# The first two row blocks of V by float32 products, in an encoder block on one core

## The chip, the core and the metric

The kernel runs on one core of one Trainium2 chip. The core has five engines with queues of their own: TensorE (PE, matrix products and transposes into PSUM banks), VectorE (DVE), ScalarE (ACT), GpSimd (POOL) and SyncE (SP, which here only issues DMAs). Each engine works through its queue in order and waits at an instruction whose inputs are not there. The metric is the device time of one execution in microseconds (us), lower is better; a kernel is given by the median of several executions.

## The reference

One encoder block over 1024 tokens of 1024 channels, all float32. The input projection comes first, and only its V part is changed; Q and K come directly behind it.

```python
u = rms_norm(x, norm1_g)                    # x * rsqrt(mean(x*x) + 1e-6) * g
proj = u @ w_in                             # 1024 x 1024 by 1024 x 5120
q, k, v, cb, cc, ch, ga, gb = split(proj)   # 512, 512, 512, 3 x 512, 2 x 1024 columns
q = rms_norm(q by heads of 64, q_norm_g)
k = rms_norm(k by heads of 64, k_norm_g)
y_a = neighbourhood_attention(q, k, v, rpb) @ w_attn_branch
y_b = short_gated_conv(cb, cc, ch, conv_w) @ w_conv_branch
x = x + (sigmoid(ga) * y_a + sigmoid(gb) * y_b) @ w_o
x = x + square(relu(rms_norm(x, norm2_g) @ w_mlp_in)) @ w_mlp_out
```

## The kernel before

**Numbers in two parts.** Every float32 operand of a product is scaled by a power of two and split into two float16 parts, a high part and the remainder, the low part. A product is then three f16 passes (`PASSES`, HH, HL, LH: high by high, high by low, low by high); low by low is left out. For the weights, ACT makes the high part from the raw tile with a per-partition scale (in `v_part`, L555, for V; in `Chunk.prep`, L306, for all others) and DVE the low part (L297 for the chunks). The scale is a power of two from the largest magnitude of the weights, or from the sum of their squares: `v_scale`, `pow2`, `pow2_half`. ACT's squares of the weights for that sum are at L266.

**The normalised input.** `x` is read in eight blocks of 128 rows (`load_x`, L366). For a block, `norm` lets ACT square it and add up along the row (L433), `rstd` makes the inverse root: DVE forms the mean (`tensor_scalar`), ACT takes `Sqrt`, and four DVE steps follow (a reciprocal and one Newton step, the last at L415). Then the high part `u[:, 0]` is made, by POOL for blocks 1 to 7 (L437) and by ACT for block 0 (L439), and the low part by DVE. `u` must lie with channels on the partitions for the products; that tile is `uT` ([128, 2, 8, 1024] f16: part, channel block, token). Blocks 0 to 2 get there by PE transposes of f16 tiles (`turn_row`, L525, eight per part, into a PSUM bank, then a copy by ACT or DVE); blocks 3 to 7 by one transposing DMA each (`ln_turn`, L444), issued by SP.

**The V stage.** V's weights are two halves of 256 columns (`cV[0]`, `cV[1]`). For blocks 0 to 2 the products are of 128 x 256 (`v_mms`, L571), 24 for a block and a half, interleaved by hand with the steps that make their operands (the order at L585 to L720: `ln_step(b)` advances the norm of a block by one step, `v_part` makes weight parts, `tick` and `step` advance the background and foreground work). `v_post` (L579) moves a finished bank to `vT`. Blocks 3 to 7 are units of 24 products of 128 x 512 (`v_unit`, issued at L210 by `unit`; its evacuation by ACT at L516). `units[0]` counts finished units, and `apart(mark)` holds back a step of the background work until so many units are issued.

**Behind it.** Sixteen units follow, Q for blocks 0 to 7 and K for blocks 0 to 7, each 24 products of 128 x 512 at L210. The evacuation of each is `qk_vec`: ACT copies it with a scale (L736), ACT squares, `rstd` (its `Sqrt` at L407), DVE products, an f16 split. Meanwhile the parts of the next weights are made. `sforms` prepares sums for a later stage (the gates): for each pair of x blocks (n, n + 4) ACT scales both with their inverse root (L482) and POOL makes four sums of 128 x 512 (L486), sixteen in all; ACT then makes their f16 high part (L491) and DVE the low part. `SFORM` lists which pair comes at which unit count. Behind these stand conv, attention, the gates, the output projection and the MLP, none of which the change touches.

**Queues and buffers.** SP's queue holds, in order, the loads of x, of the raw weights (`load_upto`, five raw buffers) and the transposing DMAs. PSUM has three `d`, three `s` and two `o` banks. At the start ACT runs one `Sqrt` on a single column, `warm`, which loads the table of that function (L371).

Of the kernel before, what the change touches and what calls it, by code (L numbers as in the profile page):

```python
# [18 lines left out]
D = 1024  # L19
# [33 lines left out]
def encoder_block(ctx: ExitStack, tc: tile.TileContext, x, weights, cols, gqk, rel, masks, out):  # L53
# [25 lines left out]
    sc = base.tile([128, 512], F32, name="sc")  # L79
    sci = sc.bitcast(I32)  # L80
    area = {"keep": [0, 0, 144], "prep": [144, 144, 240], "tmp": [240, 240, 512]}
# [163 lines left out]
    class Chunk:  # L245
# [9 lines left out]
        def prep(self):  # L255
# [5 lines left out]
            if self.kind in "QKCG":  # L261
                self.parts = wsp.tile([128, 2, tot], F16, name="w16_ws", tag="ws")
                for p, (k, w) in enumerate(self.widths):
                    while len(self.raw) <= p:
                        yield WAIT
                    A.activation(self.parts[:, 1, :k * w].bitcast(BF16), self.raw[p][:, :k * w], AF.Square,  # L266
                                 accum_out=sc[:, at(rm, p)])
# [103 lines left out]
    A.activation(sc[:, warm], sc[:, warm], AF.Sqrt)  # L371
# [14 lines left out]
    ident = w1p.tile([128, 128], F16, name="ident", bufs=1)  # L386
    G.iota(idi, pattern=[[1, 128]], base=0, channel_multiplier=-1)
    V.tensor_scalar(ident, idi, 0.0, None, op0=OP.is_equal)
# [40 lines left out]

    def norm(xin, sq, u, y, pool):  # L430
# [4 lines left out]
        yield from rstd(ss, D, y, 9)  # L435
# [35 lines left out]
    turned, formed = [0], [0]  # L471
    SFORM = ((6, 0, 0), (7, 1, 0), (9, 2, 0), (9, 0, 1), (10, 3, 0), (10, 1, 1), (12, 2, 1), (13, 3, 1))

    def sforms():

        for mark, n, split in SFORM:
            yield from apart(mark, 0)
            pair = xt[:, n:n + 5:4]
            if not split:
                assert turned[0] >= n + 5  # L480
# [15 lines left out]
    def sform_store(n, v):  # L496
        yield from apart(units[0], 1)
        A.dma_start(GS[:, n], v)
        formed[0] = n + 1
# [10 lines left out]

    def v_unit(b, ticks):
        ps = bank("ds"[b % 2])

        def post():
# [4 lines left out]
                        for k in range(8) for sa, sw in PASSES]), post, 0, ticks)  # L519

    def turn_row(b, s):

        pt = bank16("o")
        for k in range(8):
            T.transpose(pt[:, k * 128:(k + 1) * 128], u16[:, b, s, k * 128:(k + 1) * 128], ident)  # L525

        def copy():
            o, i = UT[:, s, :, b * 128:(b + 1) * 128], pt.rearrange("p (k t) -> p k t", k=8)
            if s == 0:
                A.activation(o, i, AF.Copy)  # L530
            else:
                V.tensor_copy(o, i)
        return copy
# [5 lines left out]
    def v_sum(ch, c):  # L539
        ch.sum = bank("o")  # L540
# [8 lines left out]
    def v_part(ch, s, ks):  # L549
        for k in ks:  # L550
# [5 lines left out]
            else:  # L556
                V.scalar_tensor_tensor(lo, raw, c, hi, op0=OP.mult, op1=OP.subtract)
                if k % 4 == 3:
                    done[0] += 1
                    if ch.half == 0:  # L560
                        load_upto(done[0] + 5)

    vps, vn = {}, {}

    def v_mms(b, j, ks, *passes):
        if (b, j) not in vps:
            vps[b, j], vn[b, j] = bank("ds"[b % 2 if b < 2 else j]), 0
        for k in ks:
            for sa, sw in passes:
                n = vn[b, j] = vn[b, j] + 1  # L570
                T.matmul(vps[b, j][:, :256], UT[:, sa, k, b * 128:(b + 1) * 128],  # L571
                         vhome[0][:, j, sw, k * 256:(k + 1) * 256], start=n == 1, stop=n == 24)
        if n == 24:
            units[0] += 1

    def v_post(b, j, s):
        hi, lo = (VT[:, b, w, 256 * j:256 * j + 256] for w in range(2))
        if s == 0:
            A.activation(hi, vps[b, j][:, :256], AF.Copy, scale=2.0 ** -20)  # L579
        else:  # L580
            V.scalar_tensor_tensor(lo, vps[b, j][:, :256], 2.0 ** -20, hi, op0=OP.mult, op1=OP.subtract)
# [10 lines left out]
    ln_step(0, 7)  # L592
    for k, n in (0, 4), (4, 2), (6, 2):
        V.tensor_reduce(sc[:, at(v0.rm, k, n)], v0.raw[k // 4][:, k % 4 * 256:(k % 4 + n) * 256].rearrange(
            "p (k w) -> p k w", k=n), axis=AX, op=OP.max, apply_absolute_value=True)
    turn_row(0, 0)()
    mul(v0.rm, g1, v0.rm)
    V.tensor_reduce(sc[:, v0.a], sc[:, v0.rm], axis=AX, op=OP.max, apply_absolute_value=True)
    c = ones_col()
    V.tensor_copy(c, sc[:, v0.a])  # L600
    v_sum(v0, c)
    ln_step(1)
    v_scale(v0, 1e-30, pow2(v0.b, 14, v0.s, v0.inv, False, v0.more))
    ln_step(0)
    v_part(v0, 0, range(3))
    ln_step(1)
    v_part(v0, 0, range(3, 8))
    ln_step(1, 5)
    v_mms(0, 0, (0, 1), HH)
    turn_row(0, 1)()  # L610
    v_part(v0, 1, lower)
    v_mms(0, 0, range(2, 7), HH)
    copy = turn_row(1, 0)
    v_mms(0, 0, (7,), HH)
    copy()
    v_mms(0, 0, eight, LH)
    v_mms(0, 0, lower, HL)
    ln_step(2)
    ln_step(1)
    v_mms(1, 0, eight, HH)  # L620

    def v1_square(p):
        A.activation(v1.parts[:, 1, 1024 * p:1024 * p + 1024].bitcast(BF16), v1.raw[p], AF.Square,
                     accum_out=sc[:, at(v1.rm, p)])

    v_part(v0, 1, (4,))
    ln_step(2)
    v1_square(0)
    v1_square(1)
    ln_step(3)  # L630
    v_part(v0, 1, (5,))
    ln_step(2, 5)
    turn_row(1, 1)()
    v_mms(0, 0, (4, 5), HL)
    v_mms(1, 0, range(6), HL)
    v_part(v0, 1, (6, 7))
    v_mms(1, 0, eight, LH)
    copy = turn_row(2, 0)
    V.tensor_reduce(sc[:, v1.a], sc[:, at(v1.rm, 0, 2)], axis=AX, op=OP.add)
    c = ones_col()  # L640
    V.tensor_tensor(c, sc[:, v1.a], sc[:, gm2], op=OP.mult)
    v_sum(v1, c)
    v_mms(0, 0, (6, 7), HL)
    v_mms(1, 0, (6, 7), HL)
    copy()
    v_scale(v1, 1e-36, pow2_half(v1.b, 14, v1.s, v1.inv, v1.more))
    v_part(v1, 0, lower)
    ln_step(2)
    v_mms(2, 0, eight, HH, HL)
    ln_step(3)  # L650
    v_part(v1, 0, (4, 5))
    v_part(v1, 1, (0, 1))
    copy = turn_row(2, 1)
    ln_step(3, 5)
    copy()
    v_part(v1, 0, (6, 7))
    for b in 0, 1:
        v_mms(b, 1, lower, HH, LH)
    v_mms(2, 0, eight, LH)
    v_mms(2, 1, lower, HH, LH)  # L660
    v_part(v1, 1, (2, 3))
    ln_step(4)
    v_post(0, 0, 0)
    v_post(1, 0, 0)
    ln_step(3)
    ln_turn(u16[:, 3], 3, UT)
    push(cQ)
    ln_step(4)
    v_part(v1, 1, (4, 5))
    tick()  # L670
    ln_step(5)
    ln_step(4, 5)
    for b in range(3):
        v_mms(b, 1, upper, HH, LH)
    v_part(v1, 1, (6, 7))
    v_post(2, 0, 0)
    v_post(0, 0, 1)
    ln_step(4)
    ln_turn(u16[:, 0], 4, UT)
    load_upto(8)  # L680
    turned[0] = 5
    ln_step(5)
    tick()
    ln_step(6)
    v_post(1, 0, 1)
    v_post(2, 0, 1)
    ln_step(5, 5)
    tick()
    for ks in lower, (4, 5), (6, 7):
        for b in range(3):  # L690
            v_mms(b, 1, ks, HL)
    ln_step(6)
    ln_step(5)
    ln_turn(u16[:, 1], 5, UT)
    load_upto(done[0] + 5)
    turned[0] = 6
    ln_step(7)
    for b in range(3):
        v_post(b, 1, 0)
        v_post(b, 1, 1)  # L700
    ln_step(6, 5)
    tick()
    ln_step(7)
    ln_step(6)
    ln_turn(u16[:, 2], 6, UT)
    turned[0] = 7
    ln_step(7, 5)
    tick()
    fg.append(qk_gain())
    fg.append(sforms())  # L710
    step(2)
    for b in range(3, 8):
        v_unit(b, 8)
        if b == 3:
            ln_step(7)
            ln_turn(u16[:, 3], 7, UT)
            turned[0] = 8
        step(2)
    settle()
# [1224 lines left out]
```

## Time and profile before

| what | value |
|---|---|
| median of 3 executions | 1207.19 us (1207.16 to 1207.37) |
| span of the profiled execution | 1205.3 us |
| own time of the profiled execution | not listed; the median lies 1.9 us above the span |
| PE busy | 1188.0 us, 99% |
| DVE busy | 938.7 us, 78% |
| ACT busy | 759.8 us, 63% |
| POOL busy | 433.1 us, 36% |

The profile is one execution, in microseconds from its start. Its page gives the busy time of each engine, the span in forty slices (each digit is the busy share in tenths; PEclk is the clock granted to PE, in tenths of full speed), the chain of work that ended last, and the costliest groups of instructions. The timeline lists each engine's instructions by line, operation and tiles; `out<-in` names the tiles, `x24` says that 24 like instructions are taken together, and the brackets give the idle time of the engine just before and what ended it.

### The profile page before, as it was taken

How to read it: one execution, taken by the hardware profiler on the slowest of the kernel's cores; microseconds unless marked ns; L12 is line 12 of the kernel's file. 1: busy time of each engine (PE TensorE's matmuls, PEld its weight loads, DVE VectorE, ACT ScalarE, POOL GpSimd, SP SyncE). 2: the span in 40 equal slices, each digit the busy share in tenths (PEclk: the TensorE clock that was granted, in tenths of full speed). 3: DMA queues.
4: the chain of work that ended last, by engine and by line, in shares of the span. 5: the costliest groups of instructions: out<-in, count | busy, mean ns of one | idle time of the engine just before them, and what ended most of it. 6: DMA issues, size and time to landing. Idle time of an engine off the chain costs nothing.

```text
span 1205.3 us, 17076 instructions
## 1 busy us (share of the span) xinstructions
PE 1188.0 (99%) x6294; PEld 573.8 (48%) x6294; DVE 938.7 (78%) x1759; ACT 759.8 (63%) x1183; POOL 433.1 (36%) x280
## 2 busy tenths in 40 slices
PE   6999999999999999999999999999999999999998
PEld 4444445555444444444467444444444444444444
DVE  7777988988368787877878655545548999999997
ACT  7766679867554545337779778678676744746440
POOL 1640011222311112001004465565567471553662
PEclk9999999999999999999999999999999999999999
DMA  7766657676542211224386545445465925334202
GB/s 264 151 213 141 140 119 130 133 146 123 103 123 65 67 56 53 70 93 187 57 155 183 182 159 192 149 139 193 145 247 201 352 97 217 129 138 194 105 35 105
DMA packets 171012, 173.36 MB, mean 144 GB/s; under 512 B 131504, under 2 KB 132016, under 8 KB 166832
## 3 DMA queue, kind: packets, MB, share of 16 engines
q1 hardware_dynamic: 170352, 168.07, 47.9%
q10 hardware_dynamic: 576, 4.19, 0.8%
q8 instruction: 49, 0.80, 0.3%
q14 instruction: 35, 0.29, 0.1%
HBM read 102.51 MB, written 37.75 MB: 116 GB/s over the span
## 4 chain that ended last, share of the span: by engine, by line
PE 73%; DVE 9%; ACT 1%; issue 1%; DMA 1%; DVEq 0%; ACTq 0%
PE ps_d L210 26%; PE ps_s L210 23%; PE ps_o L210 16%; PE ps_d L1039 6%; DVE w_s L1163 2%; PE ps_o L1016 1%; PE ps_s L959 1%; DVE sg L1279 1%; DVE P L999 1%; DMA u2T<-v 1%; DVE sz L973 1%; ACT w_s L1167 0%; DVE sc L317 0%; DVE m L1281 0%; ACT sg L1245 0%
## 5 line engine op out<-in xcount | busy, mean ns | idle before, releaser
L210 PEld LDWEIGHTS <-ops 128*128 128x128 f16 x1356 | 132.4, 98 | 157.3
L210 PEld LDWEIGHTS <-w 128*128 128x128 f16 x1368 | 132.8, 98 | 140.0 <-DMA u2T<-v 0.6
L1039 PE MATMUL ps_d<-uT,w_ws 128*128 128x512 f16 x528 | 123.7, 379 | 0.1
L210 PE MATMUL ps_d<-ops 128*128 128x512 f16 (+1 forms) x528 | 118.3, 374 | 0.0
L1765 ACT ACTIVATE ops<-hf,sc 128x2048 f16<-128x2048 f32 x26 | 52.0, 2000 | 97.9 <-PE ps_o L210 35.2
L210 PE MATMUL ps_s<-ops 128*128 128x512 f16 x492 | 112.9, 379 | 0.0
L1152 POOL TENSOR_TENSOR tsum<-raw 128x512 f32<-128x512 f32 x28 | 46.0, 1658 | 149.6 <-ACT raw L1138 141.6
L1345 POOL TENSOR_TENSOR as<-as 128x512 f32<-128x512 f32 x56 | 77.5, 1384 | 39.3 <-ACT as L1625 36.0
L210 PEld LDWEIGHTS <-w_s 128*128 128x128 f16 x588 | 56.8, 98 | 69.4 <-DVE w_s L1163 1.9
L210 PE MATMUL ps_d<-u2x,w 128*128 128x512 f16 (+1 forms) x360 | 80.0, 372 | 0.0
L210 PEld LDWEIGHTS <-uT 128*128 128x128 f16 x504 | 49.0, 98 | 59.6 <-DMA uT<-u 0.8
L1039 PEld LDWEIGHTS <-w_ws 128*128 128x128 f16 x528 | 51.2, 98 | 54.5 <-DVE cv L861 0.4
L210 PE MATMUL ps_o<-ops 128*128 128x512 f16 x336 | 77.1, 379 | 0.0
L1767 DVE SCALAR_TENSOR_TENSOR ops<-hf,sc,ops 128x2048 f16<-128x2048 f32 x26 | 74.0, 2846 | 3.7 <-ACT ops L1765 3.7
L210 PE MATMUL ps_o<-u2T,w 128*128 128x512 f16 (+1 forms) x324 | 71.7, 371 | 0.0
L1138 ACT ACTIVATE raw<-raw,sc 128x256 f32<-128x256 f32 x172 | 71.0, 493 | 0.8 <-DMA raw<-in_weights 0.7
L1152 POOL TENSOR_TENSOR gsum<-raw 128x512 f32<-128x512 f32 x14 | 19.0, 1376 | 133.0 <-issue 72.8
L1167 ACT ACTIVATE w<-raw,sc 128x512 f16<-128x512 f32 (+1 forms) x28 | 24.6, 927 | 54.1 <-DVE sc L426 54.1
L297 DVE SCALAR_TENSOR_TENSOR w_ws<-raw,sc,w_ws 128x512 f16<-128x512 f32 (+2 forms) x72 | 51.2, 763 | 4.7 <-ACT w_ws L306 4.7
L1658 DVE TENSOR_TENSOR as<-ps_d,as 128x512 f32<-128x512 f32 (+1 forms) x14 | 9.4, 672 | 55.8 <-ACT as L1677 53.4
L210 PE MATMUL ps_s<-u2T,w 128*128 128x512 f16 (+1 forms) x252 | 52.7, 359 | 0.0
L982 ACT ACTIVATE sz<-sz,sc 128x384 f32<-128x384 f32 (+1 forms) x64 | 37.2, 582 | 22.5 <-DVE sc L973 15.0
(357 smaller groups left out, 2629.5 us busy)
## 6 DMA issues: line engine op xcount, KB each, us to landing
raw<-in_weights SPq DMA_DIRECT2D x88, 512.0 KB, 5.4
hs<-as SPq DMA_DIRECT2D x16, 1792.0 KB, 8.7
hf<-hs SPq DMA_DIRECT2D x26, 1024.0 KB, 6.3
w2x<-in_weights SPq DMA_DIRECT2D x16, 512.0 KB, 8.1
raw<-in_weights SPq DMA_DIRECT2D x16, 384.0 KB, 3.5
xt<-in_x SPq DMA_DIRECT2D x8, 512.0 KB, 10.0
gs<-s ACTq DMA_DIRECT2D x4, 1024.0 KB, 4.0
x<-in_x SPq DMA_DIRECT2D x8, 512.0 KB, 9.8
```

Of the source, the lines that this page charges most:

```text
L210: T.matmul(ps, l, r, start=a, stop=b)
L297: V.scalar_tensor_tensor(lo, self.raw[p][:, o:o + m], sc[:, c:c + 1], hi, op0=OP.mult, op1=OP.subtract)
L959: T.matmul(ps[:, :nb * 128], QD[:, p, e, w, i * 128:(i + 1) * 128], KD[:, 2 * p + e, lo * 128:(lo + nb) * 128], start=w == 0, stop=w == 1)
L982: A.activation(z, z, AF.Exp, scale=-1.0, bias=sc[:, d["mx"]], accum_out=sc[:, d["sm"]])
L1039: T.matmul(ps, l, r, start=a, stop=b)
L1138: A.activation(v, v, AF.Copy, scale=sc[:, at(g, 4 * i + k)])
L1152: G.tensor_tensor(t[:, o], a, b, op=OP.add)
L1163: V.scalar_tensor_tensor(o(1), w, sc[:, s], o(0), op0=OP.mult, op1=OP.subtract)
L1167: A.activation(o(0), w, AF.Copy, scale=sc[:, s])
L1345: sub.tensor_tensor(z[o], z[a], z[b], op=op)
L1765: A.activation(P[:, 1, 0], hf, AF.Copy, scale=sc[:, Rs])
L1767: V.scalar_tensor_tensor(P[:, 1, 1], hf, sc[:, Rs], P[:, 1, 0], op0=OP.mult, op1=OP.subtract)
```

## The change

Row blocks 0 and 1 of V no longer need the normalised, split input. Since `u = x * r * g` with one `r` per row and one `g` per channel, `u @ W = r * ((x * g) @ W)`. PE transposes the raw float32 blocks x0 and x1 (`native_turn`: eight transposes per block with a float32 identity; the copy out of PSUM multiplies by `g1`, ACT for all of block 0 and half of block 1, DVE for the other half). `native` then multiplies them by the raw float32 weights, eight products of 128 x 256 for a block and a half, with no parts and no passes. The row factor enters in `v_post`, as the scale of the evacuation. The transposed raw blocks `xT` lie in the memory of `uT`, in a float32 view, in those token columns that are written last.

All eight blocks of `uT` now come from transposing DMAs, in the order 2 to 7, 0, 1; the f16 transposes on PE are gone. Blocks 2 to 7 are V units of 128 x 512; that of block 2 runs its HL passes last. The inverse root of a row is made by POOL, with a `pow` of -0.5 (`rpow`), where `rstd` was; `rstd` stays for the norms of Q and K. The high parts of `u` are made by ACT for all blocks (`BYPOOL` is empty). The warm-up on ACT is a `Square`, so `Sqrt` comes first with the first Q norm. The loads of x5, x6 and x7 stand on SP behind the transposing DMAs of blocks 2 and 3. `SFORM` takes the pairs in the order 2, 3, 0, 1. The weight sum of Q is held back by one unit instead of two.

```diff
-                yield from apart(units[0], 2 if self.kind == "Q" else 3)
+                yield from apart(units[0], 1 if self.kind == "Q" else 3)
...
-    A.activation(sc[:, warm], sc[:, warm], AF.Sqrt)
+    A.activation(sc[:, warm], sc[:, warm], AF.Square)
+    minus_half = keep()
+    G.memset(sc[:, minus_half], -0.5)
     load_x(0)
     SP.dma_start(sc[:, consts], cols)
     load_upto(2)
     load_x(1)
+    load_x(2)
     load_upto(4)
-    load_x(2)
     load_x(3)
-    load_upto(5)
+    load_x(4)
...
-    for b in range(4, 8):
-        load_x(b)
...
+    def rpow(ss, n, y, top):
+        v = tmp()
+        G.tensor_scalar(sc[:, v], sc[:, ss], 4.0 ** -top / n, 4.0 ** -top * EPS, op0=OP.mult, op1=OP.add)
+        G.tensor_tensor(sc[:, y], sc[:, v], sc[:, minus_half], op=OP.pow)
+        yield
...
-        yield from rstd(ss, D, y, 9)
+        yield from rpow(ss, D, y, 9)
...
-    ln = [norm(xt[:, b], sq, u16[:, b % 4], at(ys, b), b > 0) for b in range(8)]
+    BYPOOL = ()
+    ln = [norm(xt[:, b], sq, u16[:, b % 4], at(ys, b), b in BYPOOL) for b in range(8)]
...
-    SFORM = ((6, 0, 0), (7, 1, 0), (9, 2, 0), (9, 0, 1), (10, 3, 0), (10, 1, 1), (12, 2, 1), (13, 3, 1))
+    SFORM = ((7, 2, 0), (7, 3, 0), (8, 0, 0), (9, 1, 0), (9, 2, 1), (10, 3, 1), (11, 0, 1), (12, 1, 1))
...
+    def turn_row(b):
+        ln_turn(u16[:, b % 4], b, UT)
+        turned.add(b)
...
+        order = [(k, p) for k in range(8) for p in PASSES]
+        if b == 2:
+            order.sort(key=lambda o: o[1] == HL)
...
+    xT = [UT.bitcast(F32)[:, b, :, 0:128] for b in range(2)]
+
+    def native_turn(b):
+        pts = [bank("o") for _ in range(2)]
+        for k in range(8):
+            T.transpose(pts[k // 4][:, k % 4 * 128:k % 4 * 128 + 128], xt[:, b, k * 128:(k + 1) * 128], identf)
+        for k in range(4 if b else 8):
+            A.activation(xT[b][:, k], pts[k // 4][:, k % 4 * 128:k % 4 * 128 + 128], AF.Copy, scale=sc[:, at(g1, k)])
+        if b:
+            V.tensor_tensor(xT[b][:, 4:], pts[1].rearrange("p (k t) -> p k t", k=4),
+                            sc[:, at(g1, 4, 4)][:, :, None].to_broadcast([128, 4, 128]), op=OP.mult)
+
+    def native(b, j, ks):
...
+        for k in ks:
+            T.matmul(vps[b, j][:, :256], xT[b][:, k], cV[j].raw[k // 4][:, k % 4 * 256:k % 4 * 256 + 256],
+                     start=k == 0, stop=k == 7)
...
         if s == 0:
-            A.activation(hi, vps[b, j][:, :256], AF.Copy, scale=2.0 ** -20)
+            raised[b, j] = tmp()
+            V.scalar_tensor_tensor(sc[:, raised[b, j]], sc[:, at(ys, b)], 2.0 ** -20, sc[:, cV[j].s],
+                                   op0=OP.mult, op1=OP.mult)
+            A.activation(hi, vps[b, j][:, :256], AF.Copy, scale=sc[:, raised[b, j]])
```

The new order by hand, from the first transposes to the last unit of V (some lines of weight sums are left out):

```diff
+    native_turn(0)
+    for k, n in (0, 4), (4, 2), (6, 2):
+        largest(v0, k, n)
+    v_largest(v0)
+    native(0, 0, lower)
...
+    native_turn(1)
+    native(0, 0, upper)
+    native(1, 0, eight)
+    ln_step(2, 2)
...
+    native(0, 1, eight)
+    ln_step(2)
+    turn_row(2)
+    ln_step(3, 2)
...
+    load_x(5)
+    load_x(6)
+    load_upto(5)
+    v_part(v0, 0, upper)
+    ln_step(3)
+    ln_step(4, 2)
+    native(1, 1, eight)
+    ln_step(3)
+    turn_row(3)
+    v_part(v1, 0, eight)
+    v_part(v0, 1, upper)
+    load_x(7)
+    load_upto(7)
...
+    turn_row(4)
+    load_upto(8)
+    push(cQ)
+    for b in 0, 1, 5:
+        ln_step(b, 2)
...
+    v_unit(2, 0)
+    ln_step(5)
+    turn_row(5)
...
+    v_unit(3, 0)
+    ln_step(6)
+    turn_row(6)
+    ln_step(7, 3)
+    tick(2)
+    ln_step(7)
+    turn_row(7)
     fg.append(qk_gain())
     fg.append(sforms())
+    ln_step(0)
+    tick(2)
+    ln_step(0)
+    turn_row(0)
     step(2)
-    for b in range(3, 8):
+    for b in range(4, 8):
         v_unit(b, 8)
...
+        if b == 4:
+            ln_step(1)
+        if b == 5:
+            ln_step(1)
+            turn_row(1)
```

More of the change, by code (lines that the diff above doesn't have):

```diff
@@ L76, in anybank @@
         return bank("dsodsods"[rc[0] % 8])
-    sc = base.tile([128, 512], F32, name="sc")
+    sc = base.tile([128, 516], F32, name="sc")
     sci = sc.bitcast(I32)
-    area = {"keep": [0, 0, 144], "prep": [144, 144, 240], "tmp": [240, 240, 512]}
+    area = {"keep": [0, 0, 148], "prep": [148, 148, 244], "tmp": [244, 244, 516]}
     def cols_of(kind, n):
@@ L375, in encoder_block @@
     load_x(1)
+    load_x(2)
     load_upto(4)
-    load_x(2)
     load_x(3)
-    load_upto(5)
+    load_x(4)
     SP.dma_start(gq.rearrange("p a d -> p (a d)"), bass.AP(tensor=gqk.tensor, offset=gqk.offset,
                                                            ap=[[0, 128], [1, 2 * HD]]))
-    for b in range(4, 8):
-        load_x(b)
     idi = w1p.tile([128, 128], I32, name="idi", bufs=1)
-    ident = w1p.tile([128, 128], F16, name="ident", bufs=1)
     G.iota(idi, pattern=[[1, 128]], base=0, channel_multiplier=-1)
-    V.tensor_scalar(ident, idi, 0.0, None, op0=OP.is_equal)
+    identf = w1p.tile([128, 128], F32, name="identf", bufs=1)
+    V.tensor_scalar(identf, idi, 0.0, None, op0=OP.is_equal)
     UT = base.tile([128, 2, 8, S], F16, name="uT", tag="U")
@@ L479, in sforms @@
             if not split:
-                assert turned[0] >= n + 5
+                assert n in turned and n + 4 in turned
                 for b in (n, n + 4):
@@ L498, in sform_store @@
         A.dma_start(GS[:, n], v)
-        formed[0] = n + 1
+        formed[0] += 1
     def ln_step(b, n=1):
@@ L518, in v_unit @@
         unit(group(ps, [(UT[:, sa, k, b * 128:(b + 1) * 128], vhome[0][:, :, sw, k * 256:(k + 1) * 256])
[L519 to L533, printed above, removed]
+                        for k, (sa, sw) in order]), post, 0, ticks)
     def v_begin(ch):
@@ L559, in v_part @@
                     done[0] += 1
[L560 to L565, printed above, removed]
+    vps, raised = {}, {}
+    xT = [UT.bitcast(F32)[:, b, :, 0:128] for b in range(2)]
[9 more added lines that the diff above has]
+    def native(b, j, ks):
         if (b, j) not in vps:
-            vps[b, j], vn[b, j] = bank("ds"[b % 2 if b < 2 else j]), 0
+            vps[b, j] = bank("ds"[b])
         for k in ks:
[L569 to L573, printed above, removed]
+            T.matmul(vps[b, j][:, :256], xT[b][:, k], cV[j].raw[k // 4][:, k % 4 * 256:k % 4 * 256 + 256],
+                     start=k == 0, stop=k == 7)
+        if ks[-1] == 7:
             units[0] += 1
@@ L601, in encoder_block @@
-    v_sum(v0, c)
-    ln_step(1)
-    v_scale(v0, 1e-30, pow2(v0.b, 14, v0.s, v0.inv, False, v0.more))
[L604 to L610, printed above, removed]
-    v_part(v0, 1, lower)
[L612 to L629, printed above, removed]
-    ln_step(3)
[L631 to L649, printed above, removed]
-    ln_step(3)
[L651 to L658, printed above, removed]
@@ L659, in encoder_block @@
-    v_mms(2, 0, eight, LH)
-    v_mms(2, 1, lower, HH, LH)
-    v_part(v1, 1, (2, 3))
+        largest(v0, k, n)
+    v_largest(v0)
+    native(0, 0, lower)
+    v_sum(v0, v0.c)
+    v_scale(v0, 1e-30, pow2(v0.b, 14, v0.s, v0.inv, False, v0.more))
+    native_turn(1)
+    native(0, 0, upper)
+    native(1, 0, eight)
+    ln_step(2, 2)
+    largest(v1, 0, 4)
+    largest(v1, 4, 4)
+    v_part(v0, 0, (0, 1))
+    ln_step(2)
+    v_part(v0, 0, (2, 3))
+    v_largest(v1)
+    v_sum(v1, v1.c)
+    native(0, 1, eight)
@@ new lines, in encoder_block @@
+    ln_step(2)
+    turn_row(2)
+    ln_step(3, 2)
+    v_part(v0, 1, lower)
+    v_scale(v1, 1e-30, pow2(v1.b, 14, v1.s, v1.inv, False, v1.more))
+    load_x(5)
+    load_x(6)
+    load_upto(5)
+    v_part(v0, 0, upper)
+    ln_step(3)
+    ln_step(4, 2)
+    native(1, 1, eight)
+    ln_step(3)
+    turn_row(3)
[3 more added lines that the diff above has]
+    load_upto(7)
+    V.tensor_reduce(sc[:, gm2], sc[:, g1], axis=AX, op=OP.max, apply_absolute_value=True)
+    mul(gm2, gm2, gm2)
@@ L662, in encoder_block @@
     ln_step(4)
[L663 to L666, printed above, removed]
+    v_part(v1, 1, eight)
+    ln_step(4)
+    turn_row(4)
+    load_upto(8)
     push(cQ)
-    ln_step(4)
-    v_part(v1, 1, (4, 5))
-    tick()
-    ln_step(5)
[L672 to L681, printed above, removed]
-    ln_step(5)
@@ L683, in encoder_block @@
-    tick()
-    ln_step(6)
[L685 to L696, printed above, removed]
-    ln_step(7)
[L698 to L706, printed above, removed]
@@ L707, in encoder_block @@
-    ln_step(7, 5)
-    tick()
+    for b in 0, 1, 5:
+        ln_step(b, 2)
+    for j in range(2):
+        for b in range(2):
+            v_post(b, j, 0)
+    ln_step(5)
+    v_unit(2, 0)
+    ln_step(5)
+    turn_row(5)
+    load_upto(done[0] + 5)
+    for j in range(2):
+        for b in range(2):
+            v_post(b, j, 1)
+    ln_step(6, 3)
+    v_unit(3, 0)
+    ln_step(6)
+    turn_row(6)
+    ln_step(7, 3)
+    tick(2)
+    ln_step(7)
+    turn_row(7)
     fg.append(qk_gain())
     fg.append(sforms())
+    ln_step(0)
```

28 lines of the change are left out of this document (11 added, 17 removed).

## The prediction

> **What bounds the kernel now.** First the head of the page, with its slices:
>
> ```profile
> span 1205.3 us, 17076 instructions
> PE 1188.0 (99%) x6294; PEld 573.8 (48%) x6294; DVE 938.7 (78%) x1759; ACT 759.8 (63%) x1183; POOL 433.1 (36%) x280
> PE   6999999999999999999999999999999999999998
> ```
>
> TensorE's queue (PE) is the bound: 17.3 us of the span are idle, nearly all in the first and last slice. The span is 1205.3 us and the median 1207.19, so 1.9 us lie around it; no time of its own is listed for the profiled execution, and I make every sum against 1205.3 + 1.9 = 1207.2. As built, the instructions behind the V stage stand in the same order in both kernels, so only two things count: when the Q products start, and whether a later stage waits for work that the V stage left behind. The timeline comes next; columns: start, duration, engine, line, operation, tiles, and in brackets the idle time before it.
>
> ```profile
> 7.96 1.03 PE L525 MATMUL ps_o<-ident,u 128*128 128x128 f16 x8 [7.96 <-ACT u L439]
> 17.77 1.04 PE L571 MATMUL ps_s<-w_v,uT 128*128 128x256 f16 x8
> 18.64 0.61 PE L525 MATMUL ps_o<-ident,u 128*128 128x128 f16 x8
> 33.85 5.34 PE L210 MATMUL ps_s<-w_v,uT 128*128 128x512 f16 x24
> 39.46 5.35 PE L210 MATMUL ps_d<-w_v,uT 128*128 128x512 f16 x24 [0.28 <-DMA uT<-u]
> 60.22 5.34 PE L210 MATMUL ps_d<-w_ws,uT 128*128 128x512 f16 x24
> ```
>
> PE first works at 7.96, V unit 3 starts at 33.85, Q unit 0 at 60.22. Units 4 to 7 take (60.22 - 39.46)/4 = 5.19 us each. A row of eight includes about 0.17 us of drain at its end, so an f16 product of 256 columns costs (1.04 - 0.17)/8 = 0.11 us.
>
> Then the second chain, behind the V stage:
>
> ```profile
> 41.80 4.25 ACT L482 ACTIVATE xt<-xt,sc 128x1024 f32<-128x1024 f32 x4
> 44.62 30.94 POOL L486 TENSOR_TENSOR xt<-xt 128x512 f32<-128x512 f32 x16
> 75.59 1.91 ACT L491 ACTIVATE s<-xt 128x2048 f16<-128x2048 f32 x1 [0.63 <-POOL xt L486]
> 77.41 0.67 ACT L736 ACTIVATE qs<-ps_d,sc 128x512 f32<-128x512 f32 x1
> 101.68 5.34 PE L210 MATMUL ps_d<-w_ws,uT 128*128 128x512 f16 x24
> 102.97 2.68 DVE L297 SCALAR_TENSOR_TENSOR w_ws<-raw,sc,w_ws 128x512 f16<-128x512 f32 x4
> 106.86 5.34 PE L210 MATMUL ps_o<-w_ws,uT 128*128 128x512 f16 x24
> ```
>
> ScalarE (ACT) scales x, GpSimd (POOL) makes sixteen sums of it in 30.94 us without a break, ACT waits for the last, and only behind that stands its first evacuation of a Q unit, at 77.41, twelve us after that unit's products ended. This lag closes slowly: the low parts of the K weights end at 102.97 + 2.68 = 105.65 while K unit 0, which reads them, runs from 101.68 to 106.86. Its last two products need 0.6 us after the last part, so the slack is 106.86 - 105.65 - 0.6 = 0.6 us. A later start of the sums on POOL therefore moves the end of the kernel.
>
> **The start-up on PE.** Removed are 48 narrow transposes and 144 f16 products of 256 columns; added are 16 float32 transposes, 32 float32 products of 256 columns, and a sixth V unit of 24 products (row block 2). Rows for the new order:
>
> ```profile
> 0.74 0.39 SPq L366 DMA_DIRECT2D xt<-in_x  x1
> 4.37 1.06 ACT L433 ACTIVATE sq<-xt 128x1024 f32<-128x1024 f32 x1 [2.14 <-DMA xt<-in_x]
> 10.57 1.06 ACT L433 ACTIVATE sq<-xt 128x1024 f32<-128x1024 f32 x1 [0.52 <-DMA xt<-in_x]
> 37.86 0.36 ACT L579 ACTIVATE vT<-ps_d 128x256 f16<-128x256 f32 x1
> 28.90 6.43 SPq L444 DMA_TRANSPOSE uT<-u  x2
> uT<-u SPq DMA_TRANSPOSE x5, 5.2
> ```
>
> x0 is there at 4.37 and x1, the same sixth transfer in both kernels, at 10.57. Block 0's eight transposes, their copies and four products fit between these two, so they cost nothing; they are what PE gains at the front. From x1 on it is a sum. No float32 operation on PE stands in this trace. The lower bound of a product is the f16 row, 0.11 us. This kernel's own three f16 passes leave out the product of the two low parts, so a full one is four passes, 0.44; with the weight load of each pass unhidden, at the same length, 0.88. I take 0.44, between the ends and nearest to the work it does. [...] For the transposes the bounds are 0.61 (the row) and 2.44 us for eight; I take 1.0.
>
> Block 1's transposes end at 11.6. Twenty products (second half of block 0 for weight half 0, block 1 for half 0, block 0 for half 1) are 8.8, and 0.4 for a clock that is still low: 20.8. The copies on ACT, at most 0.36 each, run under the first four of them.
>
> Here stands the step that decides. As built, row block 2's transposing DMA waits on SP until PE has finished block 0's products with half 1, and block 1's products with half 1 wait until this DMA has landed: both touch the tile uT, though not the same columns. Median time to landing is 5.2 us, so PE idles from 20.8 to 26.0. What an idle PE does to its clock, the end of the trace shows (PEclk stands before the last two columns):
>
> ```profile
> 1198.69 2.78 PE L210 MATMUL ps_d<-ops 128*128 128x256 f16 x24
> 1201.50:1204.50 3.00, 0.00 (x0) 0.00 (x0) 0.88 (x2) 0.00 (x0) 0.00 (x0) 1.00 0.26 87
> 1204.60:1205.30 0.70, 0.00 (x0) 0.00 (x0) 0.00 (x0) 0.00 (x0) 0.00 (x0) 0.50 0.00 0
> ```
>
> Products ended at 1201.47, and at 1204.6, 3.1 us on, the granted clock was 0.50. A gap of 5.2 us is longer, so I expect half clock behind it. The transposes took 1.03 us for eight at 7.96 and 0.61 at 18.64, so the clock rose somewhere between; some four us of dense products precede it, and four us at half clock lose 2.0. The eight products left take 3.5 + 2.0: 31.5. [...]
>
> Then six V units: 31.5 + 0.2 (row 3's DMA, issued when the eight products end, lands 5.2 later, just after a unit of 5.19) + 6 x 5.19 = 62.8. Q unit 0 starts 2.6 us later than 60.22. With 0.11 a product and no cold clock the 28 products take 3.1 instead of 12.3 and it starts some 5 us earlier, not more, since row 2's DMA must then wait for its narrow parts; with 0.88 it is some 15 later.
>
> **The second chain.** SP's queue is in order: behind row 2's DMA stand x5, x6 and a Q weight, behind row 3's stand x7 and two more. Row 3's DMA is released at 31.5, and one takes 6.43/2 = 3.2 us to issue, so x7 is issued at 34.7 and, with x0's 4.37 - 0.74 = 3.6, there at 38.3. ACT is behind by then: the narrow values move to it from POOL.
>
> ```profile
> 13.97 1.12 POOL L437 TENSOR_SCALAR u<-xt,sc 128x1024 f16<-128x1024 f32 x1 [12.90 <-DVE sc L415]
> 0.24 0.10 POOL L1935 MEMSET const-float32-0.0<- 128x1 f32 x1 [0.24 <-issue]
> L439 ACT ACTIVATE u<-xt,sc 128x1024 f16<-128x1024 f32 x1 | 1.1, 1148 | 0.8 <-DVE sc L415 0.8
> L266 ACT ACTIVATE w_ws<-raw 128x1024 bf16<-128x1024 f32 x4 | 4.2, 1045 | 1.9 <-DMA raw<-in_weights 1.9
> 13.01 2.09 ACT L555 ACTIVATE w_v<-raw,sc 128x256 f16<-128x256 f32 x5
> 50.75 0.57 ACT L516 ACTIVATE vT<-ps_d 128x512 f16<-128x512 f32 x1
> 0.73 1.28 ACT L371 ACT_TABLE_LOAD   x1 [0.73 <-PEq L1935]
> 80.80 0.21 ACT L407 ACTIVATE sc<-sc 128x8 f32<-128x8 f32 x1 [1.02 <-DVE sc L406]
> L486 POOL TENSOR_TENSOR xt<-xt 128x512 f32<-128x512 f32 x1 | 1.3, 1270 | 0.0
> ```
>
> From x7 on ACT does, before its first scaling: the square of block 7 with its sum's read, 1.2; the wait for the power; the narrow copy, 1.15; four squares of Q weights, 4 x 1.045 = 4.2; block 0's narrow copy, 1.15; one V evacuation, 0.57. The power is two POOL instructions on 128x1: at least twice the memset, 0.2, at most two full tiles, 2 x 1.12 = 2.2; I take 0.8, nearer to the memset since the width is the same. Sum: 38.3 + 9.1 = 47.4 where 41.80 was. The first pair is scaled 2 x 1.06 later, so the sums on POOL start at 49.5 instead of 44.62: 4.9 later, and their 30.94 us are unchanged. So are the twelve us behind them, except for the table of Sqrt, 1.28 us, which is now loaded ahead of the first Q norm; ACT idles 1.02 there, so 0.3 stays. K unit 0 ends 4.9 + 0.3 - 0.6 = 4.6 later. PE's own lateness, 2.6, is covered by that wait. DVE loses the square-root steps and three copies; it has idle time at the start, so that brings nothing, and if it were full in the V stage the loss of cover would be the 0.7 of a copy.
>
> Forecast: 1207.2 + 4.6 = **1211.8**; without the cold clock everything behind 31.5 moves by 2.0, to 1209.8.
>
> **Rivals.** *The power is slow.* At 2.2 us instead of 0.8 the 1.4 counts about three times, since blocks 0, 1 and 5 queue on POOL ahead of 6 and 7, and ACT waits in order for each: 1211.8 + 4.2 = 1216.0. For it: no power stands in the trace, and POOL takes 1.12 for a plain product. Against: one element per partition. It decides from about 1 us on. A dear float32 product (0.6 instead of 0.44) ends at the same place, 28 x 0.16 = 4.5 on. *Cheap products, kept back.* At 0.11 to 0.25 PE starts Q early, but ACT's own work sets the sums: twelve squares at 1.05, sixteen weight parts at 2.09/5 = 0.42, six narrow copies at 1.15, four and two evacuations at 0.36 and 0.57 are 12.6 + 6.7 + 6.9 + 2.6 = 28.8, from the copies' end at about 12.5: 41.3, and 2 to 4 us of waits for powers and sums; so 43.3 to 45.3 against 41.80, less the slack: 1208.1 to 1210.1. *Faster.* The sums on POOL run at their first row's 1.27 us instead of 30.94/16 = 1.93, for instance because the other engines touch memory less then: 16 x 0.66 = 10.6 us off the chain, which is then no bound, and PE's start decides alone. This is faster from 0.35 us per product down: 28 x 0.09 = 2.5; at 0.20 the gain is 28 x 0.24 - 2.6 = 4.1: 1203.1. For it: the row of 1.27 and the earlier first product. Against: DVE has the same tiles to make, and both conditions must hold.
>
> **How the numbers follow.** Forecast 0.55 (own range 1209.3 to 1215), slow power or dear product 0.17, cheap but kept back 0.15, faster 0.13. About 0.2%, 2.4 us, can be told from no change. Faster by more: 0.13. Within: the cheap case's 0.15 and a little of the forecast, 0.18. Slower: 0.69. The range leaves out some 0.1 on each side: from 1204.6, which takes in the mild half of the faster case, to 1218.5, which takes in a power of 2.2 us but not a product of 0.88.
>
> **What would show it.** In the changed profile: a PE gap of about 5 us before the last eight float32 products, ended by the DMA of uT; those products at half clock; eight products in about 3.5 us before the gap; Q unit 0 near 62.8; the first form on POOL near 49.5 and the last at about 80; a wait of some two us or more inside K unit 0. I am wrong if the gap is missing, if a product takes far from 0.44, or if K unit 0 runs without a wait while Q starts late.

## The result, and the profile after

The changed kernel takes 1211.84 us (median of 5, 1211.48 to 1213.41) against 1207.23 in the same job: ratio 1.004, 95% interval 1.0027 to 1.0052. It is slower by 4.6 us. The profiled execution has a span of 1211.2 and took 1212.94, so its steps below add up to 5.9, not 4.6.

The head of the page after:

```profile
span 1211.2 us, 16879 instructions
PE 1192.5 (98%) x6206; PEld 575.5 (48%) x6206; DVE 937.3 (77%) x1721; ACT 766.0 (63%) x1187; POOL 431.2 (36%) x290
PE   7999999999999999999999999999999999999998
```

The first slice of PE is fuller than before (7, it was 6), and yet the span is longer: PE starts earlier and then waits. Its timeline after (line numbers are those of the changed kernel: L567 float32 transposes, L579 float32 products):

```profile
4.56 1.94 PE L567 MATMUL ps_o<-identf,xt 128*128 128x128 f32 x8 [4.56 <-DMA xt<-in_x]
9.50 1.07 PE L567 MATMUL ps_o<-identf,xt 128*128 128x128 f32 x8
12.14 3.62 PE L579 MATMUL ps_s<-raw,uT 128*128 128x256 f32 x16
15.62 3.70 PE L579 MATMUL ps_d<-raw,uT 128*128 128x256 f32 x16
23.77 6.64 PE L579 MATMUL ps_s<-raw,uT 128*128 128x256 f32 x16 [4.45 <-DMA uT<-u]
30.24 5.34 PE L210 MATMUL ps_d<-w_v,uT 128*128 128x512 f16 x24
42.17 5.35 PE L210 MATMUL ps_d<-w_v,uT 128*128 128x512 f16 x24 [1.40 <-DMA uT<-u]
62.92 3.92 PE L210 MATMUL ps_d<-w_ws,uT 128*128 128x512 f16 x16
67.72 0.81 PE L210 MATMUL ps_d<-w_ws,uT 128*128 128x512 f16 x3 [0.87 <-DVE w_ws L297]
71.07 0.59 PE L210 MATMUL ps_d<-w_ws,uT 128*128 128x512 f16 x2 [0.87 <-DVE w_ws L297]
71.50 5.34 PE L210 MATMUL ps_o<-w_ws,uT 128*128 128x512 f16 x24
107.78 5.34 PE L210 MATMUL ps_d<-w_ws,uT 128*128 128x512 f16 x24
```

A float32 product is listed as two instructions (16 for eight products). The gap of 4.45 us is there, ended by the DMA of uT. Q unit 0 starts at 62.92 and is cut into pieces, each waiting for a low part of Q's weights (L297): without them Q unit 1 would start 5.18 later, at 68.10; it starts at 71.50, 6.10 later than the 65.40 of before. K unit 0 (107.78) runs in one piece. The granted clock stands before the last two columns here:

```profile
23.77:25.00 1.23, 1.23 (x3) 0.50 0.76 306
28.00:29.00 1.00, 1.00 (x3) 0.50 0.08 25
29.00:30.00 1.00, 1.00 (x4) 0.64 0.06 16
30.00:31.00 1.00, 1.00 (x6) 1.00 0.00 0
```

Half clock from the end of the gap to about 29.7. The other engines after, from the same timeline (L489 scalings and L493 sums of x, L306 and L297 high and low parts of the weights, L420 and L421 the power, L710 the evacuation of a Q unit):

```profile
20.05 0.24 POOL L420 TENSOR_SCALAR sc<-sc 128x1 f32<-128x1 f32 x1 [2.45 <-ACT sq L439]
20.38 0.67 POOL L421 TENSOR_TENSOR sc<-sc 128x1 f32<-128x1 f32 x1
48.50 26.93 POOL L493 TENSOR_TENSOR xt<-xt 128x512 f32<-128x512 f32 x16 [9.46 <-ACT xt L489]
32.47 0.94 SPq L366 DMA_DIRECT2D xt<-in_x  x1
46.24 4.25 ACT L489 ACTIVATE xt<-xt,sc 128x1024 f32<-128x1024 f32 x4
55.23 2.17 ACT L489 ACTIVATE xt<-xt,sc 128x1024 f32<-128x1024 f32 x2
57.78 3.77 ACT L306 ACTIVATE w_ws<-raw,sc 128x512 f16<-128x512 f32 x6
80.82 0.67 ACT L710 ACTIVATE qs<-ps_d,sc 128x512 f32<-128x512 f32 x1
53.72 0.23 DVE L279 TENSOR_SCALAR sc<-sc 128x8 f32<-128x8 f32 x1
58.52 12.49 DVE L297 SCALAR_TENSOR_TENSOR w_ws<-raw,sc,w_ws 128x512 f16<-128x512 f32 x8
106.27 2.68 DVE L297 SCALAR_TENSOR_TENSOR w_ws<-raw,sc,w_ws 128x512 f16<-128x512 f32 x4
```

And from the timeline of before, the two rows that they are to be held against:

```profile
51.97 12.52 DVE L297 SCALAR_TENSOR_TENSOR w_ws<-raw,sc,w_ws 128x512 f16<-128x512 f32 x8
65.40 5.34 PE L210 MATMUL ps_o<-w_ws,uT 128*128 128x512 f16 x24
```

Before, the last low part of Q was ready at 51.97 + 12.52 = 64.49, and Q unit 0 ended at 65.40 without a wait; two products of 5.18/24 = 0.22 each still follow the last part, so the slack was 0.5 us. After, the parts start 6.55 later: 6.55 - 0.5 is the 6.1 by which Q unit 1 is late.

### The profile page after: what moved, and what is told of

Its sections match the earlier page's. It is cut to its first block, busy times and chain, and to the rows that moved or that the text cites. A ratio compares the mean times of both kernels' runs of the same rounds, so it can differ in the third digit from the quotient of the medians.

```text
span 1211.2 us, 16879 instructions
## 1 busy us (share of the span) xinstructions
PE 1192.5 (98%) x6206; PEld 575.5 (48%) x6206; DVE 937.3 (77%) x1721; ACT 766.0 (63%) x1187; POOL 431.2 (36%) x290
## 4 chain that ended last, share of the span: by engine, by line
PE 78%; DVE 4%; SPq 1%; issue 1%; ACT 1%; DMA 0%; DVEq 0%; ACTq 0%
PE ps_d L210 28%; PE ps_s L210 24%; PE ps_o L210 17%; PE ps_d L1013 7%; PE ps_o L990 1%; PE ps_s L933 1%; SPq L1084 1%; DVE w_s L1137 1%; DVE P L973 1%; DVE sg L1253 0%; DVE sz L947 0%; DMA uT<-gs 0%; ACT w_s L1141 0%; DVE sc L317 0%; DVE m L1255 0%
## 5 line engine op out<-in xcount | busy, mean ns | idle before, releaser
L297 DVE SCALAR_TENSOR_TENSOR w_ws<-raw,sc,w_ws 128x512 f16<-128x512 f32 (+2 forms) x72 | 51.1, 763 | 4.7 <-ACT w_ws L306 4.7
```

The source lines that it names most:

```text
L297: V.scalar_tensor_tensor(lo, self.raw[p][:, o:o + m], sc[:, c:c + 1], hi, op0=OP.mult, op1=OP.subtract)
```

## The experiments

### Is it TensorE's gap?

**Own tile.** The dependence between xT and uT is taken away.

```diff
-    xT = [UT.bitcast(F32)[:, b, :, 0:128] for b in range(2)]
+    xT = (lambda t: [t[:, b] for b in range(2)])(w1p.tile([128, 2, 8, 128], F32, name="xT", bufs=1))
```

> The changed kernel with one line changed: the transposed raw blocks xT get a tile of their own instead of a view of uT. Theory: the wait of TensorE for row block 2's transposing DMA is a dependence through the shared tile alone. Then the gap of 4.45 us before the last eight float32 products goes, these products run at full clock (3.45 us instead of 6.47), and V unit 2 starts near 22.8 instead of 30.24. What sets the end in the changed kernel is the low parts of Q's weights (71.0), behind ScalarE's queue; they move only as far as x5, x6 and x7 are issued earlier and ScalarE idles less: 2 to 4.4 us. Time 1207.4 to 1209.8. Rival, TensorE's front alone decides: all 7.5 us less the new waits, 1204 to 1206. Rival, the gap was covered by the later stall altogether: 1211.8 as it is, the stall in Q unit 0 growing from 3.4 to about 11.

Measured: 1210.13, ratio 1.0023 (1.0014 to 1.0033). The gap is gone and the clock stays full (the mean of the run is 0.999, and the last eight float32 products take 3.45 us, from 20.32 to 23.77), but Q unit 0 starts only at 60.22, since V units now wait for the transposing DMAs:

```profile
23.77 5.34 PE L210 MATMUL ps_d<-w_v,uT 128*128 128x512 f16 x24
30.47 5.35 PE L210 MATMUL ps_s<-w_v,uT 128*128 128x512 f16 x24 [1.35 <-DMA uT<-u]
37.78 7.04 PE L210 MATMUL ps_d<-w_v,uT 128*128 128x512 f16 x24 [1.96 <-DMA uT<-u]
60.22 2.32 PE L210 MATMUL ps_d<-w_ws,uT 128*128 128x512 f16 x10
57.21 12.50 DVE L297 SCALAR_TENSOR_TENSOR w_ws<-raw,sc,w_ws 128x512 f16<-128x512 f32 x8
```

The gain is 1.7, just under the 2 to 4.4 that were expected. The trace also bears on a rival that the next expectations name, that Q's low parts wait for the sum of Q's weights, which TensorE makes: that sum came 2.7 us earlier here (49.83 instead of 52.54), but the parts only 1.3. They stand 12.2 us behind ScalarE's first scaling (45.03), as in the changed kernel (12.3), so they follow ScalarE's queue.

**Own tile, x read early.** `load_x(5)` to `load_x(7)` stand behind `load_x(4)`.

> The own tile for xT, and x5, x6 and x7 loaded directly behind x4 instead of behind the transposing DMAs of row blocks 2 and 3. With the own tile alone TensorE waits 1.35, 1.96 and about 1.7 us for the transposing DMAs of blocks 3 to 5, two of which take 5.5 us to issue while x and weights are being read. Theory: with x read earlier these waits shrink to under 1.5 in all, Q unit 0 starts at 55 to 57 instead of 60.2, the first scaling comes 1 to 3 us earlier, and Q unit 1 starts at 67 to 69 instead of 70.2: 1207 to 1209.3. Rival: the waits are for the low parts of u, or the early reads hold back V's weights: 1209.5 to 1212.

Measured: 1210.23, ratio 1.0027 (1.0018 to 1.0036), no better than without. Its timeline:

```profile
33.71 5.35 PE L210 MATMUL ps_d<-w_v,uT 128*128 128x512 f16 x24 [0.47 <-DMA uT<-u]
55.35 0.38 PE L210 MATMUL ps_d<-w_ws,uT 128*128 128x512 f16 x1
56.78 0.81 PE L210 MATMUL ps_d<-w_ws,uT 128*128 128x512 f16 x3 [1.06 <-DVE w_ws L297]
68.95 5.34 PE L210 MATMUL ps_o<-w_ws,uT 128*128 128x512 f16 x24
55.99 12.48 DVE L297 SCALAR_TENSOR_TENSOR w_ws<-raw,sc,w_ws 128x512 f16<-128x512 f32 x8
```

Q unit 0 starts 7.6 us earlier than in the changed kernel, 4.9 earlier than with the own tile alone (1.2 of it was there already at TensorE's transposes of block 1), and then spends 13.6 us on a unit of 5.18. What TensorE gains in front, it waits for here: the low parts set the end. The waits for the DMAs shrank as expected, and Q unit 1 starts in the expected 67 to 69; but the low parts start 1.2 earlier than with the own tile alone, no more than TensorE's transposes of block 1 do (9.45 instead of 10.66), and the median misses the expected 1207 to 1209.3.

### Why are Q's low parts late?

**High parts of u on GpSimd again** (`BYPOOL = range(2, 8)`), alone and with the own tile.

> The changed kernel, with the high parts of u for row blocks 2 to 7 made by GpSimd again, as before, instead of ScalarE. Theory: ScalarE's in-order queue makes Q's weight parts late (it does six copies of 1.14 us more than it needs). The first scaling moves from 46.24 to 43 to 45, the low parts of Q's weights end 1.5 to 3 us earlier, the stall inside Q unit 0 (3.4) falls to 0.5 to 2: 1209 to 1210.4. Rival: the sum of Q's weights stands behind V unit 5 in TensorE's queue (52.54), which this edit does not move: the low parts start at 58.5 as before and the time stays at 1211.8.

> Both edits: xT in a tile of its own, and the high parts of u for row blocks 2 to 7 by GpSimd. Theory: with the gap gone, ScalarE's queue is what makes Q's weight parts late, so taking 6.8 us of copies off it is worth more here than alone: Q unit 1 starts at 65 to 67 instead of 71.5, and the time is 1204.5 to 1207. Rival, the parts are set by the arrival of x7 and of Q's weights: as with the own tile alone, 1207.4 to 1209.8.

Measured: alone 1213.65, ratio 1.0053 (1.0038 to 1.0068); with the own tile 1207.71, ratio 1.0006 (0.9996 to 1.0015). Alone it frees ScalarE in vain; rows of that run:

```profile
36.59 0.60 ACT L530 ACTIVATE vT<-ps_d 128x512 f16<-128x512 f32 x1 [3.67 <-PE ps_d L210]
38.45 1.06 ACT L439 ACTIVATE sq<-xt 128x1024 f32<-128x1024 f32 x1 [1.26 <-DMA xt<-in_x]
54.76 1.32 DVE L279 TENSOR_SCALAR sc<-sc 128x8 f32<-128x8 f32 x1
```

ScalarE now idles 3.67 and 1.26 us for TensorE and for x7, which the gap holds back. The first scaling is not earlier (47.25), against both my theory and its rival; it stands 22.6 us behind the end of the gap, 22.5 in the changed kernel. The last row shows a second cost: one small step of VectorE took 1.32 beside the sums of GpSimd, 0.23 in the changed kernel, where the sums were running as well. The low parts start 2.1 us later than there, 1.0 with the first scaling and 1.1 with this step.

With the gap gone as well, the same edit moves the first scaling to 39.82, and the time is 2.4 less than with the own tile alone. Q unit 1 starts at 66.33, as the theory had it, but the time lies above its 1204.5 to 1207 and in the rival's range.

**Sums held back** behind Q's parts.

```diff
-    SFORM = ((7, 2, 0), (7, 3, 0), (8, 0, 0), (9, 1, 0), (9, 2, 1), (10, 3, 1), (11, 0, 1), (12, 1, 1))
+    SFORM = ((9, 2, 0), (9, 3, 0), (10, 0, 0), (10, 1, 0), (11, 2, 1), (11, 3, 1), (12, 0, 1), (13, 1, 1))
```

> The changed kernel, with the marks in SFORM two units later for the first pairs (9, 9, 10, 10, splits at 11, 11, 12, 13), so that ScalarE's scalings and GpSimd's sixteen sums come behind Q's weight parts. Theory: Q's low parts are late because ScalarE scales x first and because VectorE takes 1.56 us for a part while GpSimd runs and 0.67 (the K parts) when it does not. They then start near 54 and end near 60, Q unit 0 has no stall, and TensorE gains 3.4 us there. The price: the sums start near 58 instead of 48.5 and end near 85, so that the evacuation of Q units comes some ten us later and TensorE waits for a bank or for K's parts. If this price is under 3.4: 1208.4 to 1211; if it is over: 1212 to 1217. Rival, the parts are late for the sum of the weights alone: they start at 58.5 and the stall stays.

Measured: 1216.63, ratio 1.0079 (1.0064 to 1.0094), in the upper range. Rows of it:

```profile
55.37 5.38 DVE L297 SCALAR_TENSOR_TENSOR w_ws<-raw,sc,w_ws 128x512 f16<-128x512 f32 x8
61.85 5.34 PE L210 MATMUL ps_d<-w_ws,uT 128*128 128x512 f16 x24
90.10 5.34 PE L210 MATMUL ps_o<-w_ws,uT 128*128 128x512 f16 x24 [2.18 <-ACT qs L710]
107.88 0.38 PE L210 MATMUL ps_d<-w_ws,uT 128*128 128x512 f16 x1 [2.08 <-ACT w_ws L306]
60.56 26.98 POOL L493 TENSOR_TENSOR xt<-xt 128x512 f32<-128x512 f32 x16 [22.27 <-ACT xt L489]
```

A low part takes 5.38/8 = 0.67 without a sum beside it and 12.49/8 = 1.56 with one, and Q unit 0 runs through. The sums, 12 us later, then hold up the evacuations and K's parts: this is the wait in K unit 0 that I had forecast for the changed kernel.

**Third pair later**: one mark, `(8, 0, 0)` to `(9, 0, 0)`.

> The changed kernel with one mark of SFORM moved, the third pair of x blocks from 8 to 9, so that ScalarE scales it behind Q's weight parts and not between the first two and the other six (2.17 us at 55.23). Theory: of the 6.55 us by which Q's low parts start later than before, 2.1 are this pair. They then start near 56.4 instead of 58.5, Q unit 1 starts near 69.4 instead of 71.5, and the time is 1209 to 1210.2. Rival: the evacuation of V unit 6 stands in front as well, and the parts stay where they are: 1211.8. Rival: the sums on GpSimd come later for it, and K unit 0 waits: 1211 to 1213.

Measured: 1211.47, ratio 1.0034 (1.002 to 1.0047), which is not apart from the changed kernel. The forecast 1209 to 1210.2 was missed. The parts did start earlier, 56.17, and Q unit 1 at 68.57; but TensorE then waits further on:

```profile
152.83 5.34 PE L210 MATMUL ps_o<-uT,w_ws 128*128 128x512 f16 x24 [1.17 <-ACT qs L710]
```

The parts start 10.40 us behind the first scaling (45.77), in the changed kernel 12.28: 1.9 of the 2.1 are found, and the gain is given back in part to an evacuation further on.

### The power

**Root steps again**: `yield list(rstd(ss, D, y, 9))` for `rpow`, and `Sqrt` as the warm-up.

> The changed kernel with the row norms of x by rstd again (ScalarE's Sqrt and five steps on VectorE, one behind the other without other work between), instead of GpSimd's power, and the warm-up by Sqrt. The power itself takes 0.19 to 0.24 and 0.55 to 0.68 us in the changed kernel's trace, as forecast. Theory: a norm by rstd takes VectorE about 1.2 us with its waits for ScalarE, eight times, in a stage where VectorE and ScalarE feed each other: u of row blocks 2 and 3 comes 0.5 to 1 us later, the parts of Q's weights 1 to 4 us later: 1213 to 1216. Rival: the norms have slack either way, and only Sqrt's table load moves (1.28 us ahead of the first Q norm goes): 1211 to 1212. Rival: GpSimd's power costs more than it saves: 1208 to 1211.

Measured: 1219.92, ratio 1.0106 (1.0091 to 1.0121): the root steps in this form cost 8 us, far more than I expected. ScalarE, in order, waits for VectorE's queue at each norm, 0.22 to 3.01 us:

```profile
31.44 0.20 ACT L406 ACTIVATE sc<-sc 128x1 f32<-128x1 f32 x1 [3.01 <-DVE sc L405]
41.10 0.20 ACT L406 ACTIVATE sc<-sc 128x1 f32<-128x1 f32 x1 [1.95 <-DVE sc L405]
```

The steps stand in one piece here; spread out between other work, as before the change, they might cost less, which was not tried.

### Taking the second chain away

**Sums on VectorE.** Own tile; GpSimd for u; the marks of the run with the sums held back; Q's weight sum in the middle of V unit 5; more background steps. The lines for the first three are those shown above and are left out here.

```diff
-                    G.tensor_tensor(z[o], z[a], z[b], op=op)
+                    (V if True else G).tensor_tensor(z[o], z[a], z[b], op=op)
...
+        if b == 5:
+            for o, l, r, first, last in mms[:12]:
+                T.matmul(o, l, r, start=first, stop=last)
+            work[0] += 12 * 512
+            mms, forced[0] = mms[12:], True
+            tick()
+            forced[0] = False
+        unit(mms, post, 0, ticks)
...
-        v_unit(b, 8)
+        v_unit(b, 8 + 4 * (b == 5))
...
-        unit(tok_mms(ps, actU, b, ch, 8, 512, 0), post, 4, 6 if 4 < n < 8 else 3)
+        unit(tok_mms(ps, actU, b, ch, 8, 512, 0), post, 4, 6 if n < 8 else 3)
```

> The own tile, the high parts of u for blocks 2 to 7 by GpSimd, the sum of Q's weights put into the middle of V unit 5, Q's weight parts ahead of the scalings of x (marks of SFORM two later), the sixteen sums on VectorE instead of GpSimd, and six background steps for every Q unit. Theory: the second chain (ScalarE, VectorE, GpSimd) sets the end, and it is long because VectorE's parts take 1.56 us beside GpSimd's sums instead of 0.67: sixteen sums at 0.67 are 10.7 us on VectorE, eight low parts get 7.1 us shorter, and the 25 us in which ScalarE waits for GpSimd are gone. Then Q unit 0 has no stall, K unit 0 starts at 97.5 to 100 (before: 101.68): 1203 to 1206. Rival: VectorE becomes the bound, TensorE waits for evacuations of Q units or for K's parts: 1207 to 1211.

> As the run with the sums on VectorE, and x5, x6 and x7 loaded directly behind x4. Theory: the waits for the transposing DMAs between V units go too, 2 to 3 us: 1200.5 to 1204. Rival: the second chain sets the end there already, so that the earlier units only wait in Q or K: 1203 to 1206, the same as without.

Measured: 1204.24, ratio 0.9977 (0.9967 to 0.9986), and with x read early 1201.62, ratio 0.9957 (0.9941 to 0.9974): 5.5 us faster than before. In the latter TensorE has no wait in V, Q or K:

```profile
54.15 5.34 PE L210 MATMUL ps_d<-w_ws,uT 128*128 128x512 f16 x24
95.61 5.34 PE L210 MATMUL ps_d<-w_ws,uT 128*128 128x512 f16 x24
43.37 5.39 DVE L297 SCALAR_TENSOR_TENSOR w_ws<-raw,sc,w_ws 128x512 f16<-128x512 f32 x8 [0.79 <-ACT w_ws L306]
50.73 5.64 DVE L496 TENSOR_TENSOR xt<-xt 128x512 f32<-128x512 f32 x8
```

Eight sums take 5.64 us on VectorE. Q unit 0 starts at 54.15 instead of 60.22 before, K unit 0 at 95.61 instead of 101.68, and the span is 1199.2: the whole 6.1 us arrive in it. Three runs take this apart; the order of Q's parts, GpSimd for u, the place of Q's weight sum and the background steps were not taken back one by one.

**Shared tile again**, all else as in the fastest:

> The fastest version so far (sums on VectorE, x read early, and the other edits), but with xT in the memory of uT again, as in the changed kernel. Theory: where nothing behind it waits, the gap and the half clock cost their whole length, 4.4 + 3 us and 0 to 1.4 for the next transposing DMA: Q unit 0 starts at 61.5 to 63 instead of 54.15 and the time is 1208.5 to 1211. Rival: Q's and K's parts still set the end and cover part of it: 1203 to 1207.

Measured: 1208.86, ratio 1.0009 (1.0000 to 1.0019). Q unit 0 starts 7.3 later than in the fastest:

```profile
61.46 5.34 PE L210 MATMUL ps_d<-w_ws,uT 128*128 128x512 f16 x24
```

The gap and the half clock now cost all of that, 7.2 us between the medians. In the changed kernel, where Q's parts were late, they had cost 1.7; with nothing but u put on GpSimd they had cost 5.9 (1213.65 and 1207.71), since there the gap held back ScalarE too.

**Sums on GpSimd**, all else as in the fastest:

> The fastest version so far, but with the sixteen sums on GpSimd as in the changed kernel. Theory: the sums take 25 to 27 us there against two times 5.64 on VectorE, end near 77 instead of 62.5, and ScalarE's first evacuation of Q units and the K parts come later: TensorE waits 2 to 6 us in Q units 4 to 7 and in K unit 0: 1204 to 1208. Rival: only the order (Q's parts first) counted: 1201 to 1202.5.

Measured: 1206.66, ratio 0.9994 (0.9984 to 1.0003), in the range but not where I put the waits: Q and the first K units run through, and TensorE waits later, for evacuations, as in this row:

```profile
113.28 5.34 PE L210 MATMUL ps_o<-w_ws,uT 128*128 128x512 f16 x24 [1.74 <-ACT qs L718]
```

**The kernel before with the same order behind V** (sums on VectorE, marks 10 to 14):

> The kernel before with the same order behind its V stage: sixteen sums on VectorE, behind Q's weight parts (SFORM 10, 10, 11, 11, splits at 12, 12, 13, 14, its count of units being one higher), six background steps for every Q unit. Theory: TensorE runs there without a break from 33.85 to the end of K, so these edits can give nothing: 1206.5 to 1208, and what the fastest version gains comes from its earlier V stage. Rival: the edits gain behind K too, 1202 to 1205, and the fastest version's gain isn't the change's.

Measured: 1207.69, ratio 1.0002 (0.9992 to 1.0011). These edits give the old kernel nothing; in the fastest they only let the earlier V stage through.

## Why the prediction was right in number and wrong in place

**What sets the end.** That the chain behind the V stage sets it and covers TensorE's lateness was right: moving Q unit 0 from 62.92 to 60.22 and 55.35 brought 1.7 us and nothing more. The step that failed is "K unit 0 ends 4.9 + 0.3 - 0.6 = 4.6 later". K's low parts were done at 106.27 + 2.68 = 108.95 while K unit 0 ran to 112.96; there was no wait. The wait stood eight units earlier in TensorE's queue, in Q unit 0, with a slack before of 0.5 us that I had not looked for, having taken the one unit whose slack I had computed for the tightest. By the prediction's own sign ("if K unit 0 runs without a wait while Q starts late") its account of the wait is wrong. With the measured values, the step gives less: K's parts were done 108.95 - 105.65 = 3.3 later, and 3.3 - 0.6 = 2.7, about what TensorE's own lateness would have cost.

**The size of the lateness.** x7 was issued at 32.47 (forecast 34.7) and the first scaling came at 46.24 (47.4), 4.4 later than before. To this come 2.1 us for the third pair, scaled ahead of six of Q's parts; the forecast left it out. The sum, 6.55 less the slack, is what the profiled execution shows. The median shows 4.6. That this equals the forecast's 4.6 is chance: the delay of the second chain was the right cause, but the forecast put it on another unit, with other terms.

**The sums "unchanged at 30.94".** They took 26.93 and ended at 75.43, when they had ended before (75.56); so the start at 48.50 (forecast 49.5) carried nothing to their end. Why a sum took 1.68 and not 1.93 on the average no run settles. The first Q evacuation was still 3.4 later, 80.82. Ahead of it ScalarE waits for VectorE, which makes the low parts of the sums (L500) only behind those of Q's weights, from 70.94 instead of 64.41:

```profile
74.74 1.06 ACT L266 ACTIVATE w_ws<-raw 128x1024 bf16<-128x1024 f32 x1 [4.75 <-DVE s L500]
```

**TensorE's front.** Product 3.45/8 = 0.43 (forecast 0.44); eight transposes 9.50 to 10.41, 0.9 (1.0); gap 4.45 (5.2); eight products behind it 6.47 (5.5), half clock costing 3.0 instead of 2.0; Q unit 0 at 62.92 (62.8). The rise of the clock that the forecast read from transposes of 1.03 and 0.61 us does not show in the listed clock, which is 1.00 throughout; here too the first eight transposes took 1.73 us (4.56 to 6.29) and the next eight 0.91, with a listed clock of 1.00 for both. A wait of 1.40 for row block 4's DMA was missed; block 1's transposes, done 1.2 earlier than forecast, about make up for it. The 0.43 is 3.9 times the 0.11 of an f16 product of the same size.

**The power.** 0.24 + 0.67 at 20.05, forecast 0.8; one of the eight took 1.18 + 0.55, at 25.33. The rival of a slow power is out, and so are cheap products and, with sums at 1.68, the faster case as it was put: it needed products of 0.35 or less. The way to faster was another one, with the sums off GpSimd and Q's parts ahead of them.

## What to carry to other kernels

Before costing a change by one slack, compute the slack of every unit that reads what the late engine makes, in the order in which they run. An earlier start of the bounding engine is worth only what the makers of its next operands can follow; here 6 us of it appeared only when Q's parts stood ahead of the scalings of x and the sums had left GpSimd; with the sums still there 1206.66 was reached. A buffer lent through another view can carry a wait between parts that share no byte; here it cost some 7 us as soon as nothing else hid it.

## What the runs showed of the hardware

A two-input step of VectorE (the low part of a weight) took 1.56 us beside GpSimd's sums and 0.67 without. Beside the same sums a step of 128x8 took 1.32 in one run and 0.23 in another, so not every step beside them was held up; what holds up the others no run shows. The sixteen sums took 11.3 us on VectorE (twice 5.64) and 24.9 to 30.9 on GpSimd.

The time lost to half clock varies for the same gap: eight products took 6.47, 6.53, 6.24, 6.04 and 5.14 us in five profiles with a gap of 4.4 to 4.5 us (the changed kernel, u on GpSimd, third pair later, shared tile again, sums held). Behind the gap the listed clock was 0.50, for some 6 us in the changed kernel (23.77 to 29.7) and for 3.3 with the sums held (24.31 to 27.6); what ends it no run shows.

A transposing DMA was issued in 1.9 to 5.8 us (1.91 at 33.43 in the kernel before, 5.79 with the own tile): in the run with the own tile the queue stood 5.54 at the second one while x and weights were read, and 3.86 with x read early.
